# Stored or recomputed lower parts of w_in, and three due times in a planned decoder layer

## The chip, the cores and the metric

The kernel runs on one core of a Trainium2 chip. The metric is the device time of one execution in microseconds. Five engines work side by side, each through a queue of its own in a fixed order: TensorE (PE, with its weight loads shown as PEld), VectorE (DVE), ScalarE (ACT), GpSimd (POOL) and SyncE (SP), which here issues nearly all DMAs.

## What is computed

One layer with two parallel token mixers on 2048 tokens of 1024 channels, batch 1:

```python
h = rms_norm(x, norm1_g); proj = h @ w_in          # 1024 -> 1536
u, xr, yr = proj[..., :512], proj[..., 512:1024], proj[..., 1024:]
s5_out  = s5_mixer(u, ...)       # 32 groups, 64 complex states each: scan, GELU, gated by w_glu
lru_out = rglru_mixer(xr, yr, ...)  # conv(4), gates, scan, times GELU(yr)
mix = concatenate([rms_norm(s5_out, s5_out_g), rms_norm(lru_out, lru_out_g)])
x = x + mix @ w_out                                # 1024 -> 1024
h2 = rms_norm(x, norm2_g)
x = x + (silu(h2 @ w_gate) * (h2 @ w_up)) @ w_down # 1024 -> 2816 -> 1024
return rms_norm(x, final_g)
```

## The kernel before, in words

**Precision.** A matmul of float32 operands is done as three passes of a faster format: each operand is cut into an upper part (ACT's copy to that format) and a lower part (the difference). `mm3` (L209 to L215) issues hi x hi, hi x lo and lo x hi for each of the 8 pieces of the inner dimension, so one 128x512 output tile takes 24 matmuls. In the trace a weight's parts are `whi` and `wlo`, and the moving operand is the first name behind the arrow (`actH`, `actL`; `aH`, `aL`; `xh`, `xl`).

**Weights.** `Unit` (L169 to L207) stands for one tile of a weight, 8 pieces of 128x128 in two halves. For each half it plans a load from memory (`wraw`, 18 plan-microseconds ahead of its use), and a split 6 ahead: ACT copies the upper part (L188), and DVE or POOL subtracts for the lower part (L189). The lower part can be kept in memory (`keep`, used in block 0 of the tokens) and loaded again (`kept`): then the subtract is left out, and there is a load of 256 KB per half instead (L195, `wlo<-wlc`), with ACT's copy at L200.

**Stages.** The tokens come in four blocks b = 0 to 3 of 512.
- `in_tb(b)`: input projection, 12 tiles m of w_in in the order 4, 5, 6, 7, 0, 1, 2, 3, 8 to 11 (i counts them). Convolution, gates and scan of the RG-LRU follow on DVE, ACT and POOL. Blocks 2 and 3 take 219 to 318 us and 318 to about 455 us.
- S5 works on two halves of the sequence (g = 0, 1) in 8 steps s each. A step is `s5_in` (PE: v, L808; DVE multiplies, L813 to L816; POOL adds, L817 and L818), `s5_scan` (POOL: k, L837 to L843; DVE scans, L847, and multiplies; POOL: `s_s`, L859) and `s5_out` (PE: y, L869 and L870). Each step loads its matrices `mi` (two buffers) and `mo` (one buffer). The second half runs from 408 to 569 us.
- `glu_tb(b)` gates the S5 output and mixes both groups (L301 to L303) into `aH`/`aL` (even b) or `actH`/`actL` (odd b).
- `out_pair(b0)`: output projection of a pair of blocks, 8 tiles m of w_out for each, residual added at L996, squares summed (L253, L255). After m = 7 of a block, `SumSq.finish` makes its norm: sums over ones on PE (L261, `nm<-ones`), a reciprocal root in 13 small DVE operations (L227 to L236, `nv`), a product with the unit matrix on PE (L269, `nm<-eye`), ACT's copy (L271), and a DMA to `r2d` (L272).
- `x_first` / `combos`: for k = 0 to 3 the two halves of the residual and `r2d` are loaded (`hx`, L1089 and L1091), normed (L1095, DVE), combined (L1103 to L1106, POOL and DVE) and split (L1061). These sums are the operands of the seven products of a Strassen scheme over w_gate, w_up and w_down (L1220, L1360), which fill the rest from 749.6 us. Sums of the weights are built on POOL (L1177, `ws`).

**What sets the order.** Every step is handed in with a due time, `at(t, function)`; the functions run sorted by it. t counts 0.65 per matmul piece (`PT`), so it is a ranking and no measured time. A scheduler with a timeline model then orders the instructions of each engine, so a due time that moves a little can move much.

Touched are the making of a `Unit` in `in_tb` (L734) and two due times in `out_pair` (L988 and L1004; lines of the kernel before).

Of the kernel before, what the change touches and what calls it, by code (L numbers as in the profile page):

```python
# [17 lines left out]
SEQ, DM, TB = 2048, 1024, 512  # L18
# [9 lines left out]
PT = 0.65  # L28
# [31 lines left out]
class Plan:  # L60
# [3 lines left out]
    def at(self, t, fn):  # L64
        self.ev.append((t, len(self.ev), fn))
# [14 lines left out]
def build(tc, nc, I, O, ctx):  # L80
    pl = Plan()
    at = pl.at
    PE, DV, AC, GP, SP = nc.tensor, nc.vector, nc.scalar, nc.gpsimd, nc.sync
# [33 lines left out]
    def dram(name, shape):  # L117
        return tc.dram_tile(list(shape), F32, name=name)
# [7 lines left out]
    r2d = [dram(f"r2d{i}", (2 * TB,)) for i in range(2)]  # L126
# [4 lines left out]
    wlc = dram("wlc", (12, 128, 8, 128))  # L131
# [11 lines left out]
    def acc():  # L143
        return PS.tile([128, TB], F32, tag="acc", name="acc", bufs=2)
# [11 lines left out]
    def aux(tag, bufs=1):  # L156
        return PS.tile([128, TB], F32, tag=tag, name=tag, bufs=bufs)
# [51 lines left out]
    def mm3(ps, u, ks, H, L, first, last):  # L209
        n = len(ks)  # L210
        for i, (kw, kx) in enumerate(ks):
            part = u.parts[kw // 4]
            for j, (w, x) in enumerate((("hi", H), ("hi", L), ("lo", H))):
                PE.matmul(ps, lhsT=part[w][:, kw % 4, :], rhs=r_(x(kx)),  # L214
                          start=first and i == 0 and j == 0, stop=last and i == n - 1 and j == 2)  # L215

    def chunks_of(t):
        return lambda k: t[:, k, :]
# [70 lines left out]
    def load_chunk(src, b, k, pool=A, tag="xc", bufs=4):  # L289
        t = pool.tile([128, TB], F32, tag=tag, name=tag, bufs=bufs)  # L290
        SP.dma_start(t, src[k * 128:(k + 1) * 128, b * TB:(b + 1) * TB])
        return t
# [319 lines left out]
    def in_tb(b, t0):  # L612
# [36 lines left out]
        def evac_u(m):  # L649
            us = v_us[:, m % 2, :]  # L650
            DV.tensor_tensor(out=us, in0=cur.pop(("ps", m)), in1=cur["rs"], op=ALU.mult)
            o = CB * (b % 2)
            SP.dma_start(ub[b // 2, :, 8 * m:8 * m + 8, :, o:o + CB].rearrange("t g h c -> (g h) t c"),
                         us.rearrange("p (t c) -> p t c", t=CT))

        def conv(m):
            h, i = divmod(m, 2)
            xr, xh = v_xr[i], v_xh[h]
            ps, rs = cur.pop(("ps", 4 + m)), cur["rs"]
            AC.copy(xr[:, 0:4], halo[:, m, :])  # L660
            DV.tensor_tensor(out=seq(xr[:, 4:TB + 4]), in0=nat(ps), in1=nat(rs), op=ALU.mult)

            end = [v.rearrange("p (t c) -> p t c", t=CT)[:, CT - 4:CT, CB - 1] for v in (ps, rs)]
            DV.tensor_tensor(out=halo[:, m, :], in0=end[0], in1=end[1], op=ALU.mult)
            AC.activation(out=xh[:, i, :], in_=xr[:, 4:TB + 4], func=AF.Identity,
                          bias=pc("cb", m), scale=pc("cw", 12 + m))
            for k in (2, 1, 0):
                DV.scalar_tensor_tensor(out=xh[:, i, :], in0=xr[:, 1 + k:1 + k + TB],
                                        scalar=pc("cw", 4 * k + m), in1=xh[:, i, :],
                                        op0=ALU.mult, op1=ALU.add)  # L670
            if i == 1:
                AC.copy(r_(v_hh), xh)
                GP.tensor_tensor(out=r_(v_hl), in0=xh, in1=v_hh, op=ALU.subtract)

        def gates(h):
            hh, hl = r_(v_hh), r_(v_hl)
            for i in range(2):
                m = 2 * h + i
                g = lt("ig", (128, TB))
                r = cur["r", h] = lt("r", bufs=2) if i == 0 else cur["r", h]  # L680
                for w, dst, bias in ((1, g, "bx"), (0, r[:, i, :], "ba")):
                    ps = aux("gt", 2)
                    for j, (a, x) in enumerate(((wgh, hh), (wgh, hl), (wgl, hh))):
                        PE.matmul(ps, lhsT=a[:, w, m, :], rhs=x[:, i, :], start=j == 0, stop=j == 2)
                    act(out=dst, in_=ps, func=AF.Sigmoid, bias=pc(bias, m))
                GP.tensor_tensor(out=v_xh[h][:, i, :], in0=g, in1=v_xh[h][:, i, :], op=ALU.mult)
# [25 lines left out]
        def gate_y(m):  # L712
            h, i = divmod(m, 2)
            if i == 0:
                cur["gy", h] = v_y if h else lt("gy")
            gy = cur["gy", h]
            DV.tensor_tensor(out=gy[:, i, :], in0=cur.pop(("ps", 8 + m)), in1=cur["rs"], op=ALU.mult)
            if i == 1:
                act(out=gy, in_=gy, func=AF.Gelu_apprx_tanh)

        def lru_out(h):
            gy, r = cur["gy", h], cur["T", h]
            for i in range(2):
                GP.tensor_tensor(out=gy[:, i, :].rearrange("p (t c) -> p t c", t=CT),
                                 in0=gy[:, i, :].rearrange("p (t c) -> p t c", t=CT),
                                 in1=r[:, i, :].rearrange("p (c t) -> p t c", t=CT), op=ALU.mult)
                sl.add(gy[:, i, :])
            if h == 1:
                sl.finish(rld[b])
            SP.dma_start(lrud[256 * h:256 * h + 256, b * TB:(b + 1) * TB].rearrange("(i p) t -> p i t", i=2), gy)  # L730

        t = t0
        for i, m in enumerate((4, 5, 6, 7, 0, 1, 2, 3, 8, 9, 10, 11)):
            u = Unit(t, I["w_in"][m], 8, GP if i % 3 == 2 else DV, *((wlc[m], None) if b == 0 else (None, wlc[m])))  # L734

            def prod(m=m, u=u, i=i):
                cur["ps", m] = aux("y", 2) if b == 0 and i in (2, 3) else acc()
                mm3(cur["ps", m], u, [(k, k) for k in range(8)], chunks_of(H), chunks_of(L), True, True)

            at(t, prod)  # L740
            t += 8 * PT
            if m < 4:
                at(t + 0.5, lambda m=m: evac_u(m))
            elif m < 8:
                at(t + 0.5, lambda m=m: conv(m - 4))
            else:
                at(t + 0.5, lambda m=m: gate_y(m - 8))
            if i == 3:
                at(t + 0.2, lambda: gates(0))
                t += 2.6  # L750
            if i == 5:
                at(t + 0.2, lambda: gates(1))
                t += 2.6
                at(t + 2, decay)
                at(t + 2 + 3, scan)
            if i in (9, 11):
                at(t + 1.0, lambda h=i // 11: lru_out(h))
# [133 lines left out]
    def pair(b):  # L891
        return (areaH, areaL) if b % 2 == 0 else (chunks_of(actH), chunks_of(actL))
# [76 lines left out]
    def out_bank():  # L969
        n = last["bank"] = last.get("bank", -1) + 1  # L970
        return acc() if n % 4 < 2 else aux("gt", 2)

    def out_pair(b0, t0):

        sums = {b: SumSq(8, ("sum", "sumh")[b % 2], dv=b >= NB - 2) for b in (b0, b0 + 1)}
        blocks = (b0, b0 + 1)
        order = [(m, b) for b in blocks for m in (0, 1)]  # L980
        order += [(m, b) for m in range(2, 6) for b in blocks]
        order += [(m, b) for b in blocks for m in (6, 7)]
        units = {}
        for n, (m, b) in enumerate(order):
            cur = C[b]
            t = t0 + n * 8 * PT + (32 * PT if b0 == 0 and n >= 12 else 0)
            if m not in units:
                units[m] = Unit(t, I["w_out"][m], 8, GP if m % 3 == 1 else DV)  # L988

            def prod(m=m, b=b, cur=cur, u=units[m]):  # L990
                cur["o", m] = out_bank()
                mm3(cur["o", m], u, [(k, k) for k in range(8)], *pair(b), True, True)

            def post(m=m, b=b, cur=cur):
                xc = cur.pop(("x", m))
                DV.tensor_tensor(out=xc, in0=cur.pop(("o", m)), in1=xc, op=ALU.add)  # L996
                sums[b].add(xc)
                SP.dma_start(x1d[b // 2][128 * m:128 * m + 128, TB * (b % 2):TB * (b % 2) + TB], xc)

            at(t - 5, lambda m=m, b=b, cur=cur: cur.__setitem__(("x", m), load_chunk(xT, b, m)))  # L1000
            at(t, prod)
            at(t + 8 * PT + 0.5, post)
            if m == 7:
                at(t + 8 * PT + 4.0, lambda b=b: sums[b].finish(r2d[b // 2][TB * (b % 2):TB * (b % 2) + TB]))  # L1004

    glu_tb(0, tin[3] + 64 * PT + 5.3)
    T = tP1 + 16 * PT
    glu_tb(1, T)
    T += 16 * PT
    out_pair(0, T)  # L1010

    tg = T + 96 * PT
# [552 lines left out]
```

## Time and profile before

| what | value |
|---|---|
| median of 3 runs | 2124.28 us (2120.08, 2124.28, 2125.39) |
| the profiled execution | 2121.99 us |
| its span | 2120.1 us, the other 1.9 us lie around it |
| mean granted TensorE clock | 0.962 |
| matmuls | 8600 |
| DMA | 409.41 MB, mean 193 GB/s |

Busy time is the time in which an engine executes; the difference to a stretch's length is idle time. A wait is named by who ended it (PE y L869 <- POOL s_s L859: PE's y of line 869 waited for POOL's s_s). The granted clock is a share of the full one: where it is 0.5, consecutive matmuls of 512 columns start 0.43 us apart, at 1.0 it is 0.23 us.

### The profile page before, as it was taken

To read this page: it belongs to the slowest core of one execution; us is meant where nothing else is said; L and a number is where in the kernel's file an instruction comes from. 1 tells how busy PE (TensorE), PEld (TensorE's weight loads), DVE (VectorE), ACT (ScalarE), POOL (GpSimd) and SP (SyncE) were. 2 spreads that over 40 slices of the span, in tenths; PEclk is the share of its full clock that TensorE was granted. 3 is DMA by queue.
4 is the path that set the end of the run, shared out by engine and by line. 5 is a ranking of instruction groups with operands and counts; after the bars stand their busy time and mean duration, and the time that the engine had idled before them with its cause. 6 is when DMAs were issued, how large, how long until landed. Compare 5 with 4: busy or idle time off the path is not lost.

```text
span 2120.1 us, 26001 instructions
## 1 busy us (share of the span) xinstructions
PE 1949.6 (92%) x8600; PEld 1560.2 (74%) x8600; DVE 1211.6 (57%) x1887; ACT 803.6 (38%) x1348; POOL 1030.7 (49%) x836
## 2 busy tenths in 40 slices
PE   7769898787989888999999999999999999999996
PEld 5647687665867766777777777777777888888885
DVE  8995678378356786444444554444443436654644
ACT  5556554652253242233233433322322344333331
POOL 2885456388444567564564543123123237544442
PEclk9879999897999999999999999999999999999998
DMA  8578998955635878544444664344343578754733
GB/s 319 175 261 240 265 267 265 213 184 174 175 101 177 281 236 311 181 162 145 144 161 147 202 199 147 132 135 146 129 135 134 184 262 303 269 183 135 244 99 104
DMA packets 262118, 409.41 MB, mean 193 GB/s; under 512 B 60480, under 2 KB 82272, under 8 KB 261984
## 3 DMA queue, kind: packets, MB, share of 16 engines
q1 hardware_dynamic: 261984, 407.76, 59.2%
q8 instruction: 67, 1.10, 0.2%
q14 instruction: 67, 0.55, 0.1%
HBM read 282.60 MB, written 125.06 MB: 192 GB/s over the span
## 4 chain that ended last, share of the span: by engine, by line
PE 63%; DVE 11%; DMA 11%; POOL 6%; issue 4%; ACT 4%; SPq 1%; POOLq 0%; DVEq 0%; ACTq 0%
PE acc L1220 9%; PE gt L1220 9%; PE y L1220 9%; PE acc L214 5%; PE v L1220 5%; PE nm L1220 5%; PE y L1360 4%; PE acc L1360 4%; PE gt L1360 4%; PE nm L1360 2%; PE v L1360 2%; DMA wraw<-w_in 2%; PE gt L214 1%; DMA ht<-xcd 1%; DMA hx<-r2d 1%
## 5 line engine op out<-in xcount | busy, mean ns | idle before, releaser
L1233 POOL TENSOR_TENSOR t<-t 128x512 f32<-128x512 f32 x66 | 100.9, 1529 | 344.7 <-DVE t L1259 219.4
L1060 ACT CAST whi<-ws 128x512 fp32r<-128x512 f32 x176 | 109.3, 621 | 337.1 <-PE y L1220 86.3
L214 PE MATMUL acc<-actH,whi 128*128 128x512 f32 x416 | 172.4, 416 | 36.9 <-ACT actH L295 15.6
L214 PE MATMUL acc<-actL,whi 128*128 128x512 f32 x416 | 172.9, 416 | 14.2 <-DVE actL L296 11.4
L1061 DVE TENSOR_TENSOR wlo<-ht,whi 128x512 fp32r<-128x512 f32 x112 | 107.7, 963 | 120.6 <-ACT whi L1060 118.6
L214 PE MATMUL acc<-actH,wlo 128*128 128x512 f32 x416 | 170.3, 411 | 0.0
L1060 ACT CAST whi<-ht 128x512 fp32r<-128x512 f32 x154 | 95.0, 618 | 163.3 <-PE nm L1360 74.5
L1061 DVE TENSOR_TENSOR wlo<-wraw,whi 128x512 fp32r<-128x512 f32 x88 | 75.9, 863 | 140.1 <-ACT whi L1060 140.1
L1061 DVE TENSOR_TENSOR wlo<-ws,whi 128x512 fp32r<-128x512 f32 x176 | 133.2, 757 | 33.9 <-ACT whi L1060 33.8
L1061 POOL TENSOR_TENSOR wlo<-ht,whi 128x512 fp32r<-128x512 f32 x42 | 58.4, 1390 | 158.9 <-ACT whi L1060 156.7
L1220 PE MATMUL y<-xh,whi 128*128 128x512 f32 x308 | 124.3, 403 | 12.2 <-ACT t L1252 9.9
L1220 PE MATMUL acc<-xh,wlo 128*128 128x512 f32 x308 | 122.5, 398 | 9.3 <-DVE wlo L1061 9.3
L214 PEld LDWEIGHTS acc<-actH,whi 128*128 128x128 f32 x416 | 83.0, 200 | 59.8 <-ACT actH L295 16.6
L1220 PE MATMUL y<-xh,wlo 128*128 128x512 f32 x308 | 123.2, 400 | 0.1
L1220 PE MATMUL y<-xl,whi 128*128 128x512 f32 x308 | 122.7, 398 | 0.0
L1220 PE MATMUL gt<-xh,wlo 128*128 128x512 f32 x308 | 121.4, 394 | 1.3 <-DVE wlo L1061 1.3
L1220 PE MATMUL acc<-xh,whi 128*128 128x512 f32 x308 | 122.1, 396 | 0.0
L1220 PE MATMUL acc<-xl,whi 128*128 128x512 f32 x308 | 122.0, 396 | 0.0
L1220 PE MATMUL gt<-xh,whi 128*128 128x512 f32 x308 | 121.6, 395 | 0.0
L1220 PE MATMUL gt<-xl,whi 128*128 128x512 f32 x308 | 121.5, 395 | 0.0
L1060 ACT CAST whi<-wraw 128x512 fp32r<-128x512 f32 x88 | 54.6, 621 | 152.2 <-PE y L1220 52.8
L214 PEld LDWEIGHTS acc<-actL,whi 128*128 128x128 f32 x416 | 83.1, 200 | 37.0 <-DVE actL L296 16.4
(464 smaller groups left out, 5463.3 us busy)
## 6 DMA issues: line engine op xcount, KB each, us to landing
td<-t SPq DMA_DIRECT2D x154, 256.0 KB, 2.1
ht<-td SPq DMA_DIRECT2D x154, 256.0 KB, 3.0
wraw<-w_down SPq DMA_DIRECT2D x99, 256.0 KB, 4.8
wraw<-w_in SPq DMA_DIRECT2D x96, 256.0 KB, 5.7
scd<-ws SPq DMA_DIRECT2D x88, 256.0 KB, 2.2
ws<-scd SPq DMA_DIRECT2D x88, 256.0 KB, 2.6
wlo<-wlc SPq DMA_DIRECT2D x72, 256.0 KB, 5.8
xc<-xT SPq DMA_DIRECT2D x56, 256.0 KB, 4.1
```

Of the source, the lines that this page charges most:

```text
L214: PE.matmul(ps, lhsT=part[w][:, kw % 4, :], rhs=r_(x(kx)), start=first and i == 0 and j == 0, stop=last and i == n - 1 and j == 2)
L1060: AC.copy(hi, raw)
L1061: eng.tensor_tensor(out=lo, in0=raw, in1=hi.bitcast(F32), op=ALU.subtract)
L1220: PE.matmul(ps, lhsT=a[:, k, :], rhs=x, start=j in FIRST and k == 0 and i == 0, stop=k == 3 and i == 2, skip_group_check=True)
L1233: (DV if q == 0 else GP).tensor_tensor(out=g, in0=c, in1=g, op=ALU.mult)
L1360: PE.matmul(BK[p][i], lhsT=a[:, i, :], rhs=x, start=j in FIRST and s == 0 and v == 0, stop=s == NSL - 1 and v == 2, skip_group_check=True)
```

## The change

Three edits:

1. In blocks 2 and 3, every third tile of w_in (i = 0, 3, 6, 9, that is m = 4, 7, 2, 9, all with their subtract on DVE) computes its lower part again instead of loading it. 16 of the 72 loads L195 go, 16 subtracts L189 come.
2. In `out_pair`, each tile of w_out is loaded and split 3 plan-microseconds sooner. Its matmuls keep their due time.
3. The norm of the residual is due 9 (b = 2) and 16 (b = 3) plan-microseconds after the end of m = 7 instead of 4. For b = 0 and 1 it stays at 4.

```diff
@@ in_tb
-            u = Unit(t, I["w_in"][m], 8, GP if i % 3 == 2 else DV, *((wlc[m], None) if b == 0 else (None, wlc[m])))
+            u = Unit(t, I["w_in"][m], 8, GP if i % 3 == 2 else DV,
+                     *((wlc[m], None) if b == 0 else (None, wlc[m]) if b == 1 or i % 3 else ()))
@@ out_pair
-                units[m] = Unit(t, I["w_out"][m], 8, GP if m % 3 == 1 else DV)
+                units[m] = Unit(t - 3.0, I["w_out"][m], 8, GP if m % 3 == 1 else DV)
@@ out_pair, after m = 7
-                at(t + 8 * PT + 4.0, lambda b=b: sums[b].finish(r2d[b // 2][TB * (b % 2):TB * (b % 2) + TB]))
+                at(t + 8 * PT + (4.0, 4.0, 9.0, 16.0)[b], lambda b=b: sums[b].finish(r2d[b // 2][TB * (b % 2):TB * (b % 2) + TB]))
```

The order of instructions changes on every engine from block 2 on. Line numbers of the new kernel are one higher from L735 on.

PE in S5's second half, where y of step s4 (`mo_4527` before, `mo_4529` after) meets the first matmuls of w_out for block 1 (`gt<-actH`). `nm_4395<-ones` and `nm<-eye` are the norm of block 1's S5 output; a number behind a name is the buffer's. Before:

```order
L261 MATMUL nm_4395<-ones_62,sumg_4186 128x1 x4
L869 MATMUL y_4693<-s_s_4610,mo_4527 128x128
L870 MATMUL y_4693<-u8_3996,mo_4527 128x128
L869 MATMUL y_4693<-s_s_4610,mo_4527 128x128
L870 MATMUL y_4693<-u8_3996,mo_4527 128x128
L275 MATMUL nm_4414<-eye_63,nv_4400 128x128 x4
L869 MATMUL y_4694<-s_s_4610,mo_4527 128x128
L870 MATMUL y_4694<-u8_3996,mo_4527 128x128
L869 MATMUL y_4694<-s_s_4610,mo_4527 128x128
L870 MATMUL y_4694<-u8_3996,mo_4527 128x128
L808 MATMUL v_4775<-u8_3996,mi_4737 64x128 x8
L214 MATMUL gt_4494<-actH_70,whi_4139 128x512
```

And after, from v of step s5 (`mi_4638`) on:

```order
L809 MATMUL v_4642<-u8_3998,mi_4638 64x128 x8
L275 MATMUL nm_4414<-eye_63,nv_4400 128x128 x4
L214 MATMUL gt_4496<-actH_70,whi_4116 128x512
L214 MATMUL gt_4573<-actH_70,whi_4206 128x512
L214 MATMUL gt_4496<-actL_71,whi_4116 128x512
L214 MATMUL gt_4496<-actH_70,wlo_4117 128x512
```

The matmuls of w_out for block 1, which stood behind all of y of s4, now stand ahead of it: 20 of them, then y of s4, then some 75 further w_out matmuls, and only then v of s6 and y of s5.

POOL at w_out's last tile m = 7 of block 2, whose two halves are split by `L189 wlo`. `ht` and `xl22` belong to the x combinations, `ws` to the sums of gate weights. Before:

```order
L189 TENSOR_TENSOR wlo_6288<-wraw_6211,whi_6287 128x512
L1103 TENSOR_TENSOR ht_5961<-hx_5903 128x512
L1177 TENSOR_TENSOR ws_6677<-wraw_6527,rd_6529 128x512
L1061 TENSOR_TENSOR xl22_6013<-hx_5905,xh22_6012 128x512
L189 TENSOR_TENSOR wlo_6324<-wraw_6240,whi_6323 128x512
L1106 TENSOR_TENSOR ht_5964<-hx_5905,ht_5963 128x512
```

After:

```order
L189 TENSOR_TENSOR wlo_6288<-wraw_6179,whi_6287 128x512
L1178 TENSOR_TENSOR ws_6653<-wraw_6527,rd_6529 128x512
L189 TENSOR_TENSOR wlo_6292<-wraw_6213,whi_6291 128x512
L1104 TENSOR_TENSOR ht_5967<-hx_5903 128x512
L1062 TENSOR_TENSOR xl22_6019<-hx_5905,xh22_6018 128x512
L1107 TENSOR_TENSOR ht_5970<-hx_5905,ht_5969 128x512
```

The second half's subtract has moved ahead of the combination of k = 2 (`ht`, `xl22`), which begins when its `hx` has been loaded.

On PE the sums over ones for b = 2 now stand 24 instead of 32 matmuls ahead of their product with eye, and those of b = 3 directly behind that product in both orders, with their own product 22 instead of 28 matmuls later. The sums and the product of b = 1 stand 18 to 20 matmuls later than before.

## The prediction

> **What bounds the kernel now.** I read the page first, then busy time by stretches, then TensorE's waits where it idles, then single instructions there. The page's first rows:
>
> ```profile
> span 2120.1 us, 26001 instructions
> PE 1949.6 (92%) x8600; PEld 1560.2 (74%) x8600; DVE 1211.6 (57%) x1887; ACT 803.6 (38%) x1348; POOL 1030.7 (49%) x836
> ```
>
> TensorE (PE) is busy 1949.6 of 2120.1 us, so 170.5 us is all that any reordering can win back, plus time at a reduced clock. The change doesn't touch the matmuls. The question is in which stretch PE idles, and which of those idle places the change reaches. Each row below is a stretch in us, then busy time (and instructions) of PE, PEld, DVE, ACT and POOL, the granted PE clock, the DMA share and GB/s.
>
> ```profile
> 318.00:371.00 53.00, 47.32 (x243) 37.47 (x240) 43.45 (x82) 22.70 (x38) 35.91 (x49) 0.94 0.82 265
> 371.00:424.00 53.00, 40.34 (x191) 32.59 (x190) 20.54 (x31) 32.04 (x43) 17.15 (x13) 0.84 0.99 213
> 424.00:477.00 53.00, 44.72 (x219) 35.10 (x217) 39.17 (x61) 26.52 (x45) 47.49 (x57) 0.92 0.55 184
> 477.00:530.00 53.00, 37.78 (x195) 29.66 (x196) 45.53 (x94) 14.77 (x29) 45.61 (x63) 0.79 0.60 174
> 689.00:742.00 53.00, 46.91 (x191) 37.25 (x190) 40.73 (x38) 13.66 (x23) 27.03 (x16) 0.90 0.84 281
> 742.00:795.00 53.00, 44.88 (x186) 35.02 (x185) 45.66 (x68) 24.55 (x44) 32.46 (x22) 0.90 0.72 236
> 848.00:901.00 53.00, 51.99 (x225) 41.71 (x224) 24.52 (x34) 14.48 (x24) 30.66 (x23) 1.00 0.51 181
> ```
>
> Three regimes. In 371 to 424 the DMA share is 0.99. In 424 to 530 POOL is busy 47.49 + 45.61 of 106 us while PE idles 8.28 + 15.22 us and loses clock (0.92 and 0.79). In 689 to 795 PE idles 6.09 + 8.12 us at clock 0.90, with DVE the busiest helper. From 848 on PE is all but full, so what the change can win lies before that. Whom PE waits for, 400 to 600 us and then 640 to 860 us (engine, line, waited for: total, times, longest):
>
> ```profile
> PE y L869 <- POOL s_s L859: 10.8, 3, 6.1
> PE v L808 <- DMA ub<-us: 9.5, 1, 9.5
> ...
> PE acc L1220 <- DVE wlo L1061: 9.3, 2, 8.7
> PE acc L214 <- POOL wlo L189: 4.1, 1, 4.1
> ```
>
> Of these the change reaches the S5 steps (s_s) and a split of w_out (L189). The 9.3 us at L1061 belong to the gate weights; their order on DVE, POOL and SP is the same in both kernels, so I leave them.
>
> **Part 1: lower parts computed.** The two groups concerned, the split's subtract and the load of a stored lower part:
>
> ```profile
> L189 DVE TENSOR_TENSOR wlo<-wraw,whi x44: 676/686/1787, 4.9 to 714.5; 128x512 fp32r<-128x512 f32 x44
> L195 SPq DMA_DIRECT2D wlo<-wlc x72: 319/383/2126, 91.7 to 432.8; - x72
> ```
>
> Two blocks x 4 units x 2 halves = 16 loads of 256 KB go, and 16 subtracts come on DVE. The ACT copy stays; it only moves into the split. DVE: 16 x 0.686 = 11.0 us, or 16 x 1.787 = 28.6 us at the slowest. They fall between 215 and 435 us, where DVE has idle time even in its fullest stretch (53 - 43.45 = 9.55 us in 318 to 371). Only those stuck in front of a convolution, scan or S5 multiply reach PE. I take +2 us (three subtracts on the path), from 0 to +5.
>
> A DVE operation beside a busy POOL costs more than its own time. The same subtract in two k of the x combinations, first with POOL busy, then with POOL idle:
>
> ```profile
> 728.09 1.76 DVE L1104 TENSOR_TENSOR ht<-hx 128x512 f32<-128x512 f32 x1
> ...
> 747.56 0.68 DVE L1104 TENSOR_TENSOR ht<-hx 128x512 f32<-128x512 f32 x1
> ```
>
> 1.76 against 0.68 us: that is the spread 0.686 to 1.787 again, and it is in my bounds. The Trainium skill ("SBUF — State Buffer", section "Who interferes with whom") gives a reason that speaks against this edit: VectorE with two SBUF inputs and GpSimd share a port pair that one of them holds for its whole instruction while the other stands. By that rule each added subtract could also hold POOL up, and 16 x 0.686 = 11 us of it would bring the sum below to about 2120 if all of it met POOL where it sets the pace. By the order that is not so: only block 3's last units (two to four subtracts) come after 424 us, so I keep +2.
>
> DMA: 16 x 256 KB = 4.19 MB, at the 213 GB/s of 371 to 424 it is 19.7 us of transfer, but spread over 220 us, and no wait of PE names wlc. About two of the loads stand in SP's queue ahead of the u loads behind PE's 9.5 us wait for ub; 2 x 0.262 MB / 213 GB/s = 2.5 us. I take -1.5 us, from -5 to +1.
>
> **Part 2: w_out loaded and split 3 us sooner.** By itself it adds nothing. Its load and split stand elsewhere in the queues, and the scheduler moves S5's steps around them. Two places count.
>
> First, S5's second half, at the place that the first order block of the section on the change shows. PE there in the kernel before (start, length, engine, line, operation, output and inputs, count, [idle before and releaser]):
>
> ```profile
> 475.88 1.12 PE L808 MATMUL v<-u,mi 128*64 128x128 f32 x6
> ...
> 498.77 0.80 PE L869 MATMUL y<-s_s,mo 128*128 128x128 f32 x2 [1.30 <-POOL s_s L859]
> ...
> 504.16 1.05 PE L261 MATMUL nm<-ones,sumg 128*128 128x1 f32 x8
> 511.30 0.80 PE L869 MATMUL y<-s_s,mo 128*128 128x128 f32 x2 [6.09 <-POOL s_s L859]
> ...
> 519.29 1.37 PE L808 MATMUL v<-u,mi 128*64 128x128 f32 x16 [2.55 <-DMA mi<-md]
> 520.59 1.22 PE L214 MATMUL gt<-actH,whi 128*128 128x512 f32 x2
> ...
> 525.24 0.50 PE L214 MATMUL gt<-actL,whi 128*128 128x512 f32 x1 [1.27 <-POOL actL L303]
> 525.58 0.39 PE L214 MATMUL gt<-actH,wlo 128*128 128x512 f32 x1
> 525.81 0.40 PE L214 MATMUL gt<-actH,whi 128*128 128x512 f32 x1
> ...
> 529.68 0.38 PE L870 MATMUL y<-u,mo 128*128 128x128 f32 x2
> ```
>
> From 504.16 + 1.05 = 505.2 to 529.7, 24.5 us, PE idles 6.09 + 2.55 + 1.27 = 9.9 us and runs much of the rest at half clock (the stretch's 0.79). In that time it does y of steps s4 and s5, one v, one norm and only 18 matmuls of w_out. In the new order the norm's broadcast (nm of b = 1) stands before y of s4 and not in its middle, and then 20 matmuls of w_out, y of s4, and about 75 further matmuls before y of s5. POOL has what w_out needs (the actL of L303) before step s4's s_s, and step s5 behind it. So w_out of block 1, which began at 520.59, can begin once the norm's result has been applied, and then covers the POOL time of s4 and s5. Its cover: up to y of s3 (498.77) POOL has the same work in both orders, so I leave that moment where it is; from s_s of s3 to s_s of s4 POOL has about 12 us of work in both (511.30 - 498.77 = 12.5 us between the two y). So y of s4 stays at about 511 to 514, with the 20 matmuls now ahead of it, and what PE has left to reach the point of 529.7 is about 3 to 5 us: it gets there at about 517 to 519, 11 to 13 us sooner. What is late next is y of s6: in the new order its v stands only 36 matmuls of w_out, one y and one v ahead of it. A step that nothing holds up, from its v to its s_s:
>
> ```profile
> 553.05 1.09 PE L808 MATMUL v<-u,mi 128*64 128x128 f32 x16
> ...
> 562.02 1.88 POOL L859 TENSOR_TENSOR s_s<-s_ta,s_wr 64x256 f32<-64x256 f32 x2
> ```
>
> From the end of v, 554.1, to 563.9 is 9.8 us. Against it stand 36 x 0.23 = 8.3 us of matmuls (two of them start at 525.58 and 525.81, 0.23 us apart), 1.1 us of v and a y: a little over 9.4 us, so nothing to 3 us comes back, by how much DVE and POOL are shared there. I take -10 us, from -15 to +2.
>
> Second, w_out's tile m = 7 of block 2. POOL there, and the two waits of PE:
>
> ```profile
> 725.37 2.24 POOL L1103 TENSOR_TENSOR ht<-hx 128x512 f32<-128x512 f32 x1 [5.23 <-DVE hx L1095]
> 727.58 1.72 POOL L1177 TENSOR_TENSOR ws<-wraw,rd 128x512 f32<-128x512 f32 x1
> 729.26 1.72 POOL L1061 TENSOR_TENSOR xl<-hx,xh 128x512 fp32r<-128x512 f32 x1
> 730.94 1.71 POOL L189 TENSOR_TENSOR wlo<-wraw,whi 128x512 fp32r<-128x512 f32 x1
> ...
> 727.71 0.50 PE L214 MATMUL acc<-aH,whi 128*128 128x512 f32 x1 [1.95 <-ACT whi L188]
> ...
> 732.71 0.80 PE L214 MATMUL acc<-aH,wlo 128*128 128x512 f32 x1 [4.14 <-POOL wlo L189]
> ```
>
> The second of the two splits of this tile waits in POOL's queue behind the x combination of k = 2, which itself waits for a load. In the new order it stands ahead of that combination (second order block), so these 1.95 + 4.14 = 6.1 us go, and with them half a clock: 0.10 of 53 us in 689 to 742 is 5.3 us. The Trainium skill ("TensorE: Matmul & The Clock Gate", Part 1) puts the way back to full clock at one busy window of about 3.4 us, so by it only 1.7 us per stall would be lost; the granted clock of the trace decides, and it shows 5.3. Together -11.4 us, if nothing else is late. But something is: the last piece of x for the gate matmuls, and the norm behind it, end on DVE here:
>
> ```profile
> 753.36 0.68 DVE L1061 TENSOR_TENSOR xl<-ht,xh 128x512 fp32r<-128x512 f32 x1
> 753.97 0.16 DVE L227 TENSOR_SCALAR nm<-nm 128x4 f32<-128x4 f32 x1
> ...
> 760.96 0.15 DVE L236 SCALAR_TENSOR_TENSOR nv<-nv,nm 128x4 f32<-128x4 f32 x1
> ...
> 754.49 0.40 PE L1220 MATMUL acc<-xh,whi 128*128 128x512 f32 x1
> ...
> 761.26 0.58 PE L269 MATMUL nm<-eye,nv 128*4 128x128 f32 x2 [5.91 <-DVE nv L236]
> ```
>
> The piece of x is done at 753.36 + 0.68 = 754.04 and PE uses it at 754.49, so it has almost no slack. The chain to it starts from block 1's norm (its row of r2d), which by the order stands 18 to 20 matmuls, 4 us, later against PE's work. With PE 11 us earlier it just waits at the gate matmuls. I take -1.5 us for the whole stretch 689 to 795, from -9 to +4.
>
> **Part 3: the two norms planned later.** For b = 2 the sums over ones move from 32 to 24 matmuls ahead of the product with eye, 8 x 0.23 = 1.8 us. DVE reached that norm only at 753.97, behind that piece of x, while PE had the sums 32 matmuls (7.4 us) ahead of the last one at 754.95, so the delay is covered, and the 5.9 us wait at L269 stays: its length comes from DVE's other operations between L227 and L236 (753.97 to 760.96 for a chain of 0.15 us pieces). For b = 3 the order keeps the sums where they were and only the product with eye comes 6 matmuls sooner, 1.4 us of cover. 0 us, from -2 to +2, within the bounds above.
>
> **Sum**, against the profiled execution of 2121.99 us, which lies 2.3 us below the median of 2124.28: -10 - 1.5 - 1.5 + 2 = -11, so 2111 us. A measurement of this kernel tells about 0.3% (6.4 us) from no change.
>
> **Rivals.**
> *Taken back (2120 us, 0.23).* The S5 gain goes: POOL, busy 93 of 106 us, sets when y of s3 and all after it come, DVE's added subtracts lengthen POOL's operations as in the 1.76 us row, and y of s1 to s2 now waits for mo. For it: mo has one buffer, and in the new order only 20 matmuls stand between y of s1 and y of s2. Against: POOL has no more work than before. Of -10 only -1 is left, with the other terms unchanged: 2120.
> *The whole gain (2100 us, 0.12).* The x chain follows PE instead of holding it, because it starts from w_out of blocks 0 and 1, which ends earlier too. Then -11.4 instead of -1.5: 2101. Against: the chain stands behind r2d, 4 us later in the order.
> *Slower (2135 us, 0.13).* v of S5's step s2 has moved back about 60 matmuls and now stands some 12 us of PE time before its y; s3's stands about 10 us before its y. In the kernel before, step s3 took from its last v (475.88 + 1.12) to y at 498.77, 22 us, since POOL and DVE do w_out's mixing in between. If both steps take 22 us, PE waits 10 + 12 us, less the 1.30 us it waits there now, and about 4 us at half clock: +25 against -11, 2135. It decides against the change once the two steps together exceed some 33 us (12 + 10 + 11). Against: s3 lasted so long because its v came early, in pieces between other matmuls; POOL has the same work up to y of s3.
>
> **How the numbers follow.** Forecast 0.52, whole gain 0.12, taken back 0.23, slower 0.13. "Faster" is below 2117.9: nearly all of the forecast, the whole gain, none of the others: 0.61. "Same" reaches to 2130.7: taken back and a little of the forecast: 0.26. Slower 0.13. The range runs from the whole gain with some of S5's (2099) to S5 at its upper bound of +2 with the added DVE work (2121 + 3), and a part of the way to the slower case: 2128. The forecast's own range is 2104 to 2118.
>
> **What would show it.** Right: the product with eye that now starts at 761.26 comes about 11 us sooner; PE busy in 477 to 530 at 44 us or more; no wait for s_s of 6 us; no wait for L188 or L189 at w_out's m = 7, and in its place a wait for xl or xh of the x combinations before the first gate matmuls; the 5.9 us at L269 still there. Wrong: a wait for s_s or mo of several us at steps s2 or s3, w_out of block 1 still beginning after 518, or a new wait in 318 to 371, where DVE is fullest.

## The result and the profile after

| | median | ratio to the kernel before |
|---|---|---|
| before | 2122.78 us (2118.06 to 2130.23) | |
| changed | 2112.45 us (2106.07 to 2116.55) | 0.9942, 95% interval 0.9925 to 0.9959 |

By the ratio the change makes the kernel 12.3 us faster (0.0058 x 2122.78), between 8.7 and 15.9. The quotient of the two medians alone is 0.9951, 10.3 us, inside the same interval. The forecast was -11 us, 2111. The page of the changed kernel's profiled execution:

```profile
span 2104.0 us, 25991 instructions
PE 1945.5 (92%) x8600; PEld 1556.2 (74%) x8600; DVE 1214.0 (58%) x1903; ACT 803.2 (38%) x1348; POOL 1032.2 (49%) x836
```

The same stretches as before (PE, PEld, DVE, ACT, POOL busy, PE clock, DMA share, GB/s):

```profile
424.00:477.00 53.00, 44.28 (x228) 35.51 (x229) 42.19 (x78) 30.67 (x50) 48.20 (x52) 0.94 0.51 169
477.00:530.00 53.00, 41.84 (x211) 32.71 (x210) 39.40 (x77) 14.79 (x27) 46.03 (x62) 0.90 0.69 197
...
689.00:742.00 53.00, 47.00 (x204) 36.71 (x202) 43.66 (x47) 16.08 (x28) 29.76 (x18) 0.98 0.86 296
742.00:795.00 53.00, 47.59 (x184) 35.90 (x185) 39.75 (x61) 22.57 (x41) 35.99 (x25) 0.86 0.83 269
```

In 477 to 530 PE is busy 41.84 instead of 37.78 us, at clock 0.90 instead of 0.79, while POOL works as much as before (46.03 against 45.61): the same work of POOL now has more of PE's work beside it. In 689 to 742 PE's idle time is all but the same, 6.00 against 6.09 us, but its clock is 0.98 instead of 0.90; of that gain of clock, half is lost again in 742 to 795, where it is 0.86 instead of 0.90. The 16 subtracts and loads have changed places in their two groups:

```profile
L189 DVE TENSOR_TENSOR wlo<-wraw,whi x60: 661/686/1791, 5.0 to 707.2; 128x512 fp32r<-128x512 f32 x60
L195 SPq DMA_DIRECT2D wlo<-wlc x56: 319/382/1905, 92.0 to 427.2; - x56
```

S5's second half on PE (start, length, engine, line, operation, count, [idle before and releaser]):

```profile
494.55 0.80 PE L870 MATMUL y<-s_s,mo 128*128 128x128 f32 x2 [6.21 <-POOL s_s L860]
...
497.98 1.09 PE L809 MATMUL v<-u,mi 128*64 128x128 f32 x16
499.01 1.16 PE L275 MATMUL nm<-eye,nv 128*128 128x128 f32 x8
502.70 0.74 PE L214 MATMUL gt<-actH,whi 128*128 128x512 f32 x2 [2.54 <-ACT actH L302]
...
511.07 0.38 PE L870 MATMUL y<-s_s,mo 128*128 128x128 f32 x2
...
533.32 0.46 PE L870 MATMUL y<-s_s,mo 128*128 128x128 f32 x2 [1.48 <-DMA mo<-md]
```

Directly behind v of s5 come the norm (499.01) and, after 2.54 us, w_out of block 1 (502.70 instead of 520.59). y of s4 starts at 511.07, without a wait, where the prediction had 511 to 514. The wait of 6 us for s_s isn't gone, though: it now stands one step sooner, at y of s3 (6.21).

At w_out's m = 7 POOL has the second subtract (715.19) ahead of the x combination (718.62):

```profile
715.19 1.75 POOL L189 TENSOR_TENSOR wlo<-wraw,whi 128x512 fp32r<-128x512 f32 x1
718.62 2.21 POOL L1104 TENSOR_TENSOR ht<-hx 128x512 f32<-128x512 f32 x1 [1.68 <-DVE hx L1096]
```

PE's next waits are for x and the norm:

```profile
734.94 0.50 PE L1221 MATMUL y<-xh,whi 128*128 128x512 f32 x1 [1.44 <-ACT xh L1061]
738.87 0.50 PE L1221 MATMUL y<-xl,whi 128*128 128x512 f32 x1 [1.57 <-DVE xl L1062]
741.99 0.80 PE L1221 MATMUL acc<-xh,whi 128*128 128x512 f32 x1 [2.16 <-ACT xh L1061]
744.70 0.79 PE L1221 MATMUL acc<-xl,whi 128*128 128x512 f32 x1 [1.91 <-DVE xl L1062]
748.65 0.58 PE L269 MATMUL nm<-eye,nv 128*4 128x128 f32 x2 [2.74 <-DVE nv L236]
```

7.1 us of new waits for xh and xl stand where the 6.1 us of waits for L188 and L189 shrank to one of 0.63 us, and the norm's wait is 2.74 instead of 5.91 us. PE takes up the norm 12.6 us sooner (748.65 against 761.26).

### The profile page after: what moved, and what is told of

Same layout as the page of the kernel before. It is cut to its first block, busy times and chain, and to the rows that moved or that the text cites. A ratio compares the mean times of both kernels' runs of the same rounds, so it can differ in the third digit from the quotient of the medians.

```text
span 2104.0 us, 25991 instructions
## 1 busy us (share of the span) xinstructions
PE 1945.5 (92%) x8600; PEld 1556.2 (74%) x8600; DVE 1214.0 (58%) x1903; ACT 803.2 (38%) x1348; POOL 1032.2 (49%) x836
## 4 chain that ended last, share of the span: by engine, by line
PE 58%; DMA 3%; DVE 3%; issue 2%; POOL 2%; ACT 1%; SPq 0%; POOLq 0%; DVEq 0%; ACTq 0%
PE gt L1221 9%; PE acc L1221 9%; PE y L1221 9%; PE y L1361 5%; PE v L1221 5%; PE acc L1361 5%; PE nm L1221 5%; PE gt L1361 5%; PE v L1361 2%; PE nm L1361 2%; DMA hx<-r2d 1%; DMA ht<-xcd 1%; DVE wlo L1062 1%; POOL r L1393 1%; ACT t L1253 1%
## 5 line engine op out<-in xcount | busy, mean ns | idle before, releaser
L214 PE MATMUL acc<-actH,whi 128*128 128x512 f32 x416 | 171.2, 414 | 33.4 <-ACT actH L295 10.3
```

What stands on the lines that cost most here:

```text
L214: PE.matmul(ps, lhsT=part[w][:, kw % 4, :], rhs=r_(x(kx)), start=first and i == 0 and j == 0, stop=last and i == n - 1 and j == 2)
```

## The experiments

Every kernel was timed against the kernel before on the same chip; the last four rows are from another chip than the eight from part 1 to part 1 in block 2 only. Beside the ratio stand three marks of its profiled execution, in us: the start of y of S5's last step, of the product with eye for b = 2 (761.26 before), and the span.

| kernel | ratio, 95% interval | last y | L269 | span |
|---|---|---|---|---|
| before | | 567.05 | 761.26 | 2120.1 |
| changed | 0.9942 (0.9925 to 0.9959) | 554.91 | 748.65 | 2104.0 |
| part 1 | 1.0002 (0.9988 to 1.0015) | 557.20 | 753.04 | 2117.9 |
| part 2 | 0.9995 (0.998 to 1.001) | 563.71 | 753.76 | 2116.5 |
| part 3 | 1.0005 (0.9992 to 1.0019) | 563.02 | 755.91 | 2114.3 |
| parts 1 and 2 | 0.9978 (0.9961 to 0.9995) | 558.73 | 748.71 | 2111.5 |
| changed, again | 0.9947 (0.9927 to 0.9968) | 558.29 | 748.17 | 2106.0 |
| parts 1 and 3 | 0.9965 (0.9951 to 0.998) | 559.50 | 755.39 | 2114.1 |
| parts 2 and 3 | 0.9966 (0.9952 to 0.9979) | 561.70 | 753.08 | 2109.7 |
| part 1 in block 2 only | 1.0023 (1.0008 to 1.0037) | 569.32 | 765.07 | 2131.6 |
| part 1, one tile | 0.9951 (0.9933 to 0.997) | 554.44 | 750.29 | 2109.8 |
| part 1, one subtract of w_down on DVE | 0.9985 (0.9967 to 1.0004) | 557.09 | 754.24 | 2111.5 |
| one tile, parts 2 and 3 | 0.9915 (0.9886 to 0.9944) | 553.92 | 744.58 | 2103.0 |
| changed, norms later still | 0.9963 (0.9945 to 0.9981) | 561.01 | 754.16 | 2118.5 |

A mark of one execution isn't sharp. Up to 700 us the kernel with part 3 alone is the kernel before, instruction for instruction, and its last y still stands 4.0 us sooner. Nor does the profiled execution always lie near the median of its kernel: 2106.07 against 2112.45 us for the changed kernel, 2116.16 against 2122.75 for part 3, 2133.37 against 2126.29 for part 1 in block 2 only, 2120.43 against 2112.84 for the norms later still. So marks are read over several kernels, and times by the ratios.

### Each part alone, and parts 1 and 2

The prediction put S5's new order down to part 2. The order of the kernels with one part shows it with part 1 instead; theory B took that up.

```diff
# part 1 alone: only the edit in in_tb.   part 2 alone: only the edit of Unit(t - 3.0, ...)
# part 3 alone: only the edit of the norm's due time.   parts 1 and 2: the changed kernel with
-                at(t + 8 * PT + (4.0, 4.0, 9.0, 16.0)[b], lambda b=b: sums[b].finish(...))
+                at(t + 8 * PT + 4.0, lambda b=b: sums[b].finish(...))
```

> The kernel before with part 1 alone (16 lower parts of w_in computed instead of loaded). In its order S5's second half already stands as in the changed kernel: w_out of block 1 ahead of y of s4, y of s5 behind some 75 further matmuls; the split of w_out's m = 7 stands as in the kernel before. Theory A (as the prediction put it: the new S5 order is worth about 10 us and comes with part 2): part 1 alone costs or saves under 2 us, ratio 0.999 to 1.001. Theory B (the S5 order is worth about 10 us whoever makes it, and it is part 1 that makes it): 8 to 13 us faster at y of S5's last step, ratio 0.994 to 0.997, and PE still waits about 6 us at m = 7 for L188 and L189.

> The kernel before with part 2 alone (w_out loaded and split 3 plan-microseconds sooner). In its order S5's second half stands as in the kernel before, and both splits of m = 7 stand ahead of the x combination of k = 2. Theory A (part 2 carries the gain): ratio 0.994 to 0.996. Theory B: the 6.1 us at m = 7 and about 5 us of half clock go, and 7 to 10 of these 11 us are waited for again at the first gate matmuls and the norm, so ratio 0.998 to 1.000. Rival (the x chain follows PE): all 11 us stay, ratio 0.995.

> The kernel before with part 3 alone (two norms due later). In its order only the sums for b = 2 move, from 32 to 24 matmuls ahead of their product with eye. All theories: within 2 us, ratio 0.999 to 1.001; the wait at L269 stays at 4 to 6 us. A ratio under 0.998 would show that the norm's place frees DVE for the x combinations.

> The changed kernel without part 3 (both norms due at 4 again). If part 3 does nothing: the same as the changed kernel, ratio 0.993 to 0.996 against the kernel before. If the later norm is what lets the x chain through, PE waits longer for it at L269 (5 to 6 us instead of 2.7) and the ratio is 0.996 to 0.998.

No part alone changes the time clear of its interval. Theory A falls at once: with part 2 alone the last y stands at 563.71, as with part 3 alone (563.02). Theory B is right about the place and wrong about the time. Part 1 brings the last y to 557.20, 7 to 8 us ahead of the mean of before and part 3 alone (565.0), and still the whole time is that of before. PE's waits from 640 to 860 us with part 1 alone (engine, line, waited for: total, times, longest) show one place where the lead is spent:

```profile
PE acc L1221 <- DVE wlo L1062: 6.1, 2, 5.8
PE nm L269 <- DVE nv L236: 6.0, 2, 5.7
PE y L1221 <- DVE wlo L1062: 5.2, 1, 5.2
PE acc L214 <- ACT whi L188: 4.2, 1, 4.2
PE acc L214 <- POOL wlo L189: 3.9, 1, 3.9
```

The stall at m = 7 is there, 8.1 us against 6.1 before. With part 2 alone it is gone from the same view, and other waits have come:

```profile
PE acc L1220 <- DVE xl L1061: 2.8, 1, 2.8
PE nm L269 <- DVE nv L236: 2.5, 1, 2.5
PE acc L1220 <- ACT xh L1060: 1.9, 2, 1.3
PE nm L261 <- DVE sum L255: 1.7, 1, 1.7
```

From the last y to the product at L269 it takes 190.1 us with part 2 alone and 194.2 and 192.9 us in the two kernels with the old order and no part 2 (before, part 3 alone): 11 us of stall and half clock removed, 3 to 4 us kept by then, and nothing kept in the ratio (0.9995). Over all fourteen profiles this stretch takes 191.3 us on average in the seven with part 2 and 195.4 in the seven without, so part 2 is worth about 4 us up to the norm.

Here I had only half of it: the lead of part 1 is lost again behind 860 us too. The second place came out with the 6.13 us operation below.

### All parts again, and without one

```diff
# parts 1 and 3: the changed kernel with Unit(t, I["w_out"][m], ...) again
# parts 2 and 3: the changed kernel with the old line for u in in_tb
# part 1 in block 2 only:
+                     *((wlc[m], None) if b == 0 else (None, wlc[m]) if not (b == 2 and i % 3 == 0) else ()))
```

> The changed kernel itself, timed beside the kernels that lack one part, on the same chip. Theory C (the three parts help only together: part 1's S5 order brings PE about 8 us sooner to y of S5's last step, part 2 takes away the stall at m = 7, and part 3 lets DVE finish the x combinations and the norm sooner): ratio 0.993 to 0.996. Theory D (part 3 does nothing and the difference between the changed kernel and parts 1 and 2 is spread of the runs): ratio 0.996 to 0.998, as for parts 1 and 2.

> The changed kernel without part 2: S5's second half in the new order, the stall at m = 7 as in the kernel before. Theory C: the S5 lead of about 8 us stands at w_out of blocks 2 and 3, PE waits about 8 us at m = 7 for L188 and L189, and the ratio is 0.997 to 1.000. Theory E (the stall at m = 7 costs nothing, since what is saved there is waited for again at the first gate matmuls): the same ratio as the changed kernel, 0.993 to 0.997.

> The changed kernel without part 1: S5's second half in the old order, both splits of m = 7 sooner, both norms later. If the S5 order carries most of the gain: ratio 0.998 to 1.001, y of S5's last step within 4 us of the kernel before. If parts 2 and 3 together make the gain: ratio 0.994 to 0.997.

> The kernel before with part 1 in block 2 alone (8 loads less, 8 subtracts more on DVE). By its order S5's second half stays in the old order up to v of the last step, and m = 7 as in the kernel before, so this shows the price of the subtracts and the worth of the loads without a new order. As the prediction costed them (half of +2 and of -1.5): within 2 us, ratio 0.999 to 1.001. If the subtracts hold up POOL and DVE by their whole time: 8 x 0.7 to 8 x 1.8, 5 to 14 us slower, ratio 1.002 to 1.007. If the freed DMA is what matters: PE's wait for mo and xc in blocks 2 and 3 falls and the ratio is 0.997 to 0.999.

The ratios follow the order of theory C: 0.9947 with all parts, 0.9965 to 0.9978 with two, 1.000 with one. So each of the three edits as it stands is worth 0.2 to 0.4% beside another and nothing alone; the next section shows that for part 1 this nothing is a gain and a price. Two points of C aren't shown. Without part 2 the ratio is 0.9965, just below C's range and inside that of theory E, and its interval meets that of all parts, so E isn't ruled out. And parts 2 and 3 without part 1 have 0.9966, the range written down for the two making the gain together; their interval too meets that of all parts. The difference of part 3 is the clearest: 1.0002 to 0.9965 beside part 1, 0.9995 to 0.9966 beside part 2, 0.9978 to 0.9947 beside both. Beside part 2 its place is behind the norm: from L269 to the end of the span it takes 1355.4 and 1357.8 us in the two runs with all parts, 1356.6 us with parts 2 and 3, and 1362.8 and 1362.7 us with parts 1 and 2 and with part 2. Without part 2 there is no such difference between the kernel before (1358.8) and part 3 alone (1358.4). The wait at L269 itself doesn't depend on it: 2.5 us with part 2 alone, 2.74 with all, and 5.7 to 6.4 us in all kernels without part 2. Most of the 5 to 6 us are lost at once. The 30 us from 748 on, with all parts and then with parts 1 and 2, where L269 starts at the same time:

```profile
748.00:778.00 30.00, 28.64 (x109) 21.82 (x110) 20.59 (x35) 15.52 (x28) 17.65 (x13) 0.85 0.78 245
748.00:778.00 30.00, 25.78 (x91) 18.80 (x92) 18.69 (x32) 14.42 (x26) 13.84 (x10) 0.83 0.69 228
```

PE does 109 matmuls there with part 3 (109 in the second run of all parts too) and 91 without; 18 matmuls are 4.1 us at full clock and 7.7 at half. Without part 3 PE waits between 750 and 780 us for xh, xl and whi of the next products, 3.3 us in sum against 0.2 and 0.6 in the two runs with all parts. With part 2 alone it is 97 matmuls in the 30 us from 753 on, with parts 2 and 3 113. Why these pieces come later without part 3 stays open.

Part 1 in block 2 alone is slower, 1.0023: 8 subtracts more and 8 loads less, in the old S5 order. That is +4.9 us (1.7 to 7.8), inside the range written down for subtracts that hold up POOL and DVE by their whole time (1.002 to 1.007). But the long operation shown below stands in its profile too, so the two causes aren't separated here.

### One tile is enough

Which tile computes its lower part turns out to decide the order in an erratic way. By the order of instructions alone, one tile of block 2 or 3 (i = 0, 3 or 9 of block 2, i = 3 of block 3) brings the new S5 order; the other four single tiles and all four of block 2 together do not. Of the single tiles i = 0 of block 2 was run. That separates the order from the subtracts.

```diff
# one tile:
+                     *((wlc[m], None) if b == 0 else (None, wlc[m]) if not (b == 2 and i == 0) else ()))
# one tile, parts 2 and 3: the same line in the changed kernel
# part 1, one subtract of w_down on DVE: part 1 alone, and in w_unit
-                    G(out=r, in0=cur["a"], in1=cur["b"], op=ALU.subtract)
+                    (DV.tensor_tensor if j == 3 and s == 1 else G)(out=r, in0=cur["a"], in1=cur["b"], op=ALU.subtract)
# norms later still: in the changed kernel
-                at(t + 8 * PT + (4.0, 4.0, 9.0, 16.0)[b], ...)
+                at(t + 8 * PT + (4.0, 4.0, 14.0, 21.0)[b], ...)
```

> The kernel before with part 1 for a single tile (block 2, i = 0): 2 loads less and 2 subtracts more instead of 16. By its order S5's second half stands in the new order as with all of part 1 (w_out of block 1 ahead of y of s4). Theory F (part 1 works through the order alone): y of S5's last step 6 to 10 us sooner, as with all of part 1. Theory G (the loads taken away are what helps): two loads of 16 give an eighth, under 2 us at that y. For the whole time: m = 7's stall stays, so 0.997 to 1.000 under F, 0.999 to 1.001 under G.

> Part 1 alone, with one subtract of the last down-projection weights moved from POOL to DVE (j = 3, s = 1), the one that took 6.13 us on POOL at 1961 us with part 1 alone and at most 1.84 us with parts 2 or 2 and 3. If that long operation is what gives back 4 to 5 us of part 1's lead: PE's waits of 0.61, 0.61 and 1.14 us at 1972 to 1984 us and the half clock with them go, and the ratio falls from 1.000 to 0.997 to 0.999. If it is only a sign of something else (a late load): another POOL operation or a load is late in its place, and the ratio stays at 1.000.

> The changed kernel with part 1 cut down to that single tile. Theory F: as fast as the changed kernel or a little faster, since 14 subtracts are saved, ratio 0.991 to 0.996. Theory G: like parts 2 and 3 alone, 0.996 to 0.998.

> The changed kernel with both norms due 5 plan-microseconds later again (14 and 21). By its order the sums for b = 2 stand 4 to 7 matmuls (about 1 us) ahead of their product with eye instead of 24 (5.5 us). If a later norm helps since it leaves DVE to the x combinations: the waits for xh and xl before it (9.8 us with the norm's own wait) shrink by 2 us or more and the ratio is 0.992 to 0.995. If the norm's own chain on DVE then ends last: the wait at L269 grows from 2.7 to 5 to 8 us, ratio 0.996 to 0.998.

Theory F: with 2 subtracts instead of 16 the last y stands at 554.44, as soon as in the changed kernel, and the ratio is 0.9951, better than F had it. S5 on PE with that one tile:

```profile
497.40 2.05 PE L275 MATMUL nm<-eye,nv 128*128 128x128 f32 x8 [5.42 <-DVE nv L236]
...
504.00 0.73 PE L214 MATMUL gt<-actH,whi 128*128 128x512 f32 x2
...
511.95 0.49 PE L870 MATMUL y<-s_s,mo 128*128 128x128 f32 x2 [1.30 <-POOL s_s L860]
```

w_out begins at 504.00 and y of s4 at 511.95, like the changed kernel's 502.70 and 511.07. The loads taken away (theory G) aren't needed for it. With parts 2 and 3 beside it this is the fastest kernel of the study, 0.9915 (0.9886 to 0.9944); its interval just meets that of the whole change, 0.9925 to 0.9959, so that the 14 further subtracts cost something is likely and not shown by this pair.

The two runs with one tile say more about the sum of the change than any of the kernels with a whole part. The S5 order alone is worth 10.4 us (0.0049 x 2120.3), parts 2 and 3 together 7.2 us (0.0034 x 2120.8), which makes 17.6; with both the kernel measures 18.0 us (0.0085 x 2120.3). So the two gains add up within the noise. The whole change has only 12.3 and 11.2 us of it, which leaves some 6 us as the price of the other seven tiles. In the kernel with part 1 alone this price eats the gain: 1.0002 (0.9988 to 1.0015) against 0.9951 (0.9933 to 0.997) with one tile, intervals that lie apart. Its profile is behind that of the single tile by 2.8 us at the last y, by 2.8 at L269 and by 8.1 at the end of the span (2117.9 against 2109.8), and from 517 us on both have PE's matmuls in the same order. Most of the 5 us behind L269 are the operation shown next.

Norms due later still: the wait at L269 grows to 4.3 us, part 3's gain is not increased, 0.9963. The same view as above:

```profile
PE gt L1221 <- DVE t L1258: 7.5, 1, 7.5
PE nm L269 <- DVE nv L236: 4.3, 1, 4.3
```

So the norm's own chain ends later, as expected for that case; here, besides, a DVE operation of the next stage holds PE for 7.5 us. This execution was 7.6 us above the median of its kernel, so its waits may overstate what the ratio contains.

**The operation that gives the lead back.** Part 1 alone, at 1960 us, in the last of the down-projection products. POOL's subtract for the weights:

```profile
1961.26 6.13 POOL L1324 TENSOR_TENSOR wd<-wraw,ws 128x512 f32<-128x512 f32 x1 [3.12 <-DMA ws<-sdd]
```

DVE beside it, the first and last of a row of seven without gaps, each with two inputs from SBUF, and the next operation, one of whose inputs (`acc`) is a matmul's output in PSUM:

```profile
1961.94 0.68 DVE L1062 TENSOR_TENSOR wdl<-ws,wdh 128x512 fp32r<-128x512 f32 x1
...
1965.55 0.68 DVE L1062 TENSOR_TENSOR wdl<-ws,wdh 128x512 fp32r<-128x512 f32 x1
1966.41 0.69 DVE L1397 TENSOR_TENSOR r<-acc,r 128x512 f32<-128x512 f32 x1 [0.18 <-PE acc L1361]
```

PE's waits after it:

```profile
1973.17 0.50 PE L1361 MATMUL y<-wlo,wdh 128*128 128x512 f32 x1 [0.61 <-POOL wlo L1062]
1976.90 0.50 PE L1361 MATMUL y<-wlo,wdh 128*128 128x512 f32 x1 [0.61 <-DVE wlo L1062]
1984.05 1.05 PE L1414 MATMUL acc<-ones,t 128*128 128x1 f32 x8 [1.14 <-POOL t L1408]
```

The same instruction in the changed kernel:

```profile
1951.99 1.31 POOL L1324 TENSOR_TENSOR wd<-wraw,ws 128x512 f32<-128x512 f32 x1 [3.08 <-DMA ws<-sdd]
```

Its group with that one subtract given to DVE (ns of one, shortest/median/longest):

```profile
L1324 POOL TENSOR_TENSOR wd<-wraw,ws x10: 1407/1751/1872, 1954.3 to 2016.3; 128x512 f32<-128x512 f32 x10
```

In that kernel another POOL operation meets the end of the same row of DVE, 2.82 us long, and DVE goes on behind it without a gap:

```profile
1963.19 2.82 POOL L1062 TENSOR_TENSOR wlo<-ht,whi 128x512 fp32r<-128x512 f32 x1 [7.02 <-DMA out_dram<-r]
...
1964.17 0.68 DVE L1062 TENSOR_TENSOR wdl<-ws,wdh 128x512 fp32r<-128x512 f32 x1
1964.78 0.68 DVE L1397 TENSOR_TENSOR r<-acc,r 128x512 f32<-128x512 f32 x1
```

6.13 us against 1.31: POOL's operation lies over seven DVE operations that follow each other without a gap, and ends 1.16 us after the last of them (1967.39 against 1966.23). In the other three kernels with a long operation it is 1.17 us, and here 1.16 us again (1966.01 against 1964.85), though DVE didn't pause. So the pause of 0.18 us isn't what lets POOL go: common to all five is the end of the row with two inputs from SBUF. Why POOL isn't let in between two operations of this row, as it was 5 us earlier in a row of L1425 (1.62 us at 1956.53), stays open. SP's next weight load waits for the long operation, and two POOL operations later PE does. The order of all engines in this stretch is the same in both kernels; only the moment differs at which POOL's operation meets DVE's row. With the subtract moved to DVE the long operation and the three waits of PE are gone, and part 1 alone comes to 0.9985. The two intervals overlap (part 1 alone 0.9988 to 1.0015), so the ratio only points the way of the 3.6 us (0.0017 x 2120); the trace shows the operation and the waits themselves. The same long operation, 6.0, 6.1 and 5.6 us, stands in the profiles of part 1 in block 2 only, of parts 1 and 3, and of the norms later still, and in none of the other kernels. There is one profile of each, so whether it comes in every execution of a kernel isn't known.

## Why the prediction was right or wrong

**S5's second half: right in mechanism and place, wrong in what brings it.** The step said -10 (-15 to +2); the marks of the last y average 557 in the nine profiles with the new order (553.9 to 561.0) and 564 in the four kernels with the old order outside block 2's test (before, part 2, part 3, parts 2 and 3; 561.7 to 567.05): -7 us; the changed kernel's two profiles stand 9.0 and 5.6 us ahead of that 564, and 12.1 and 8.8 ahead of the kernel before. By the ratio of the one tile the order is worth 10.4 us. PE arrived at y of s4 at 511.07, within the window forecast, and at 514.82 in the second run. What was not foreseen is the wait at y of s3: its moment, which the prediction left where it is, 498.77, came at 494.55 and 499.20, but with 6.2 us of waiting for s_s, here and in all kernels with the whole of part 1 (6.2 to 6.9 us). "Part 2 ... the scheduler moves S5's steps around them" is the step that failed: part 1, even one tile of it, makes the new order; part 2 alone leaves the old. The order of the whole change alone could not show this; the order of each edit by itself would have.

**m = 7: right.** The -11.4 us were expected to be waited for again at the x combinations, -1.5 kept. The changed kernel's lead is 12.1 us at the last y and 12.6 at L269, in the second run 8.8 and 13.1, with 7.1 us of new waits for xh and xl; over all profiles part 2 is worth 4 us here, within the range. One detail was wrong: the 5.9 us at L269 were to stay, and became 2.7, probably since part of that wait now lies ahead of it, at xh and xl.

**The norms: mis-sized.** "0 us, from -2 to +2". Beside another part the later norm is worth 0.29 to 0.37%, 6 to 8 us. The cover that I counted, matmuls ahead of L269, plays no part in it: the wait there is 2.5 us without part 3 and 2.7 with it. Beside part 2 the gain lies behind the norm, and the prediction looked only ahead of it.

**Part 1's price, +2 - 1.5: too small.** y of S5's first step of the second half starts at 432.70 and 435.69 against 431.40, behind 12 more matmuls in the new order, and no load's absence shows as a gain. The kernels with one tile put the price of the other seven at some 6 us beside parts 2 and 3, and at 11 us (0.0051 x 2120) alone, of which 3.6 by the ratio, and about 5 in the profile, are the long operation at 1960 us. The long operation was in no term, and what makes up the rest isn't shown.

**The sum: right with luck.** -11 was forecast and -12.3 measured because two errors cancel. S5 had its size, 10.4 us for 10. Parts 2 and 3 brought 7.2 us instead of 1.5, and part 1 cost some 6 us instead of 0.5.

**The prediction's own signs.** The product with eye came 12.6 us sooner, and the waits at m = 7 gave way to waits for xh and xl, as forecast. Three signs of being right did not come: PE is busy 41.84 us in 477 to 530 and not 44, there is still a wait of 6 us for s_s, and the 5.9 us at L269 did not stay. One sign of being wrong did come, a wait for s_s of several us at step s3. The time was forecast well by steps that were only in part what happened.

**The rivals.** "Taken back" gives the time of each part by itself, but not the reason: with part 1 alone the lead stands at the last y, and is given back behind it. "Slower" named the right place, s3's y now waits 6.21 us for s_s, and too high a price: POOL had much the same work there, busy 94.2 us of 424 to 530 against 93.1.

## What to carry to other kernels

Where a scheduler sets the order, an edit's own cost and saving (here 2 or 16 subtracts) can be far smaller than the order it happens to bring; take the order of each edit by itself before saying which edit carries which term. A stall removed ahead of a chain without slack is worth what the chain's end moves, so two small edits along one chain can be worth nothing one by one (0.9995 and 1.0005 for parts 2 and 3) and 7 us together (0.9966). An edit that measures nothing can also be a gain and a price of the same size: cut it down to the least that still brings the new order, as the one tile does, and the two come apart. And when an edit's lead vanishes far downstream in an unchanged order, look for one instruction that has grown.

## What was not expected of the hardware

A GpSimd operation that took 1.31 us in the changed kernel lasted 6.13, 6.12, 6.02 and 5.64 us in four kernels while VectorE ran back-to-back operations with two inputs from SBUF, and ended 1.16 or 1.17 us after the last of them each time. The prediction had only VectorE's side of such a meeting, 0.68 against 1.76 us, and no long one on POOL's side. The Trainium skill ("SBUF — State Buffer", section "SBUF: two separate sides") has the loser of the shared port stand for the other's whole instruction; the 6.13 us are longer than one instruction of 0.68 and agree with waiting through a whole row of seven, so here the loser stood for more than one instruction.
